# A transformer trunk layer on one core: projection weights split once and kept in DRAM, and the fillers' casts tied into order

## The chip, the cores and the metric

The kernel runs on one core of one Trainium2 chip. A core has five engines that work side by side, each on its own list of instructions, in the order of that list: PE (TensorE, matmuls), DVE (VectorE), ACT (ScalarE), POOL (GpSimd) and SP (SyncE), which here issues all DMAs. An engine that reaches an instruction whose inputs are not there, or whose output place is not free, waits, and what stands behind it on that engine waits too. The metric is the device time of one execution in microseconds (us); the median of several runs is compared.

## What is computed

One layer of an encoder over 1024 positions of width 1024 in float32. A combined projection gives queries, keys and values for two branches of eight heads (64 wide) and two gates. Branch a is softmax attention over a band with a learned bias, branch b is stick-breaking attention. Each branch is projected from 512 to 1024, gated by a sigmoid, the two are added and go through an output projection. Then come a residual with layer norm, a SwiGLU feed-forward part and a second layer norm.

```python
h = x @ w_in[l]
qa, ka, va, qb, kb, vb, ga, gb = jnp.split(h, split_pts, axis=-1)
y_a = chunk_band_attention(heads_a(qa), heads_a(ka), heads_a(va), rel_bias[l]) @ w_proj_a[l]
y_b = stick_breaking_attention(heads_b(qb), heads_b(kb), heads_b(vb)) @ w_proj_b[l]
gate_a = jax.nn.sigmoid(ga + b_gate[l, :D])
gate_b = jax.nn.sigmoid(gb + b_gate[l, D:])
mix = (gate_a * y_a + gate_b * y_b) @ w_out[l]
x = layer_norm(DEEPNORM_ALPHA * x + mix, ln1_g[l], ln1_b[l])
```

## The kernel before

**Precision.** Every float32 matmul is made of three faster ones. An operand is split into a high part (a cast, always on ACT) and a low part (source minus high part, on DVE or POOL); the products high x high, high x low and low x high are added in PSUM. So a weight costs a load, a cast on ACT and a subtraction before PE can use it. `begin_w` issues the load of a weight; the function that it returns, `end`, does the cast (L441, tiles wh_...) and the subtraction (L442, tiles wl_...).

**Stage one** (to about 345 us) makes the column blocks of the combined projection in pairs ("projects" p1 to p16), each with seven products in place of eight (Strassen's scheme). Queries, keys, values and five pairs of gates go to DRAM. ACT copies each product out of its PSUM bank and adds the gates' bias and sigmoid (L398), SP stores the result (L399). `run_pairs` runs the projects and loads the weights of the next ones ahead.

**The attention** (345 to about 663 us) goes over 16 heads, eight of branch a and then eight of branch b, of 12 steps each. For a head, PE makes scores (sc, L547 and L548), ACT, DVE and POOL make weights of them (branch a: exponentials L590, scale L595 on POOL; branch b: sigmoids L622 and L623, scans L625 and L628 on DVE, product L630 on POOL), PE transposes the weights (tp, L653), ACT and DVE split them (pt, L109 and L110), and PE multiplies them with the values (pv, L666 and L667). A group of four or eight steps shares one pv bank, of which there is one; when the group's last product is made, ACT copies the bank out (L685), and the next group may begin. `pend` holds products back by LAG = 2 steps.

Since a head's chain leaves PE with gaps, other matmuls, the **fillers**, are strewn between: `fill_all` is a generator that gives one matmul at a time, and the table FILL says how many of them each head's steps take. The fillers are the gates 10 to 15 (gps, L462), each with its own weight, and then the projection of branch a's heads (yAps, L738), whose inputs y0 to y3 are read back from DRAM and split (L774 on ACT, L775 on POOL) and whose weights (wr_y0_0 to wr_y0_3, raw) are loaded, cast and split in the midst of the heads. Gates that were not squashed in stage one are squashed (sigmoid, L782) when their tile comes up.

**The merge** (to about 708 us) multiplies branch b's heads with their projection weights (yBps, L116 to L119, two banks), multiplies by the gate (L880), adds branch a's part (L881) and splits the sum (mh, ml). Then comes the output projection (ops), whose first four weights o0_0 to o0_3 are loaded, cast and split beforehand; and then the feed-forward part, which the change doesn't touch.

**Order.** The program is written in one order, and a scheduler of the tile framework makes each engine's list of it; casts of weights drift ahead of their place in the program as early as it sees fit. An instruction given to `tc.keep_in_program_order` isn't moved. Tiles lie in numbered slots by tag (`op` has 8, `gt` 3, `kp` 4, `xt` 16); a tile that takes a slot waits until the last user of the slot before is done.

## Time and profile before

| What | Value |
|---|---|
| Median of 3 runs | 1456.3 us (1455.09 to 1456.57) |
| Profiled execution | 1452.42 us, of which the span in the profile is 1450.6 us |
| PE busy | 1429.1 us (99%), 6748 matmuls |
| DVE, ACT, POOL busy | 1024.0 us (71%), 678.7 us (47%), 279.2 us (19%) |
| DMA | 246.15 MB, mean 170 GB/s |

The profile is that of one execution. Matmuls overlap one another, so PE counts as busy also where it goes at less than its pace; a 128x512 matmul shows 389 ns, but one starts every 0.23 us where PE isn't held up. Rows of the timeline give start and duration in us, engine, line, tiles, and in brackets the idle time of the engine before the row with what ended it. Line numbers are those of the kernel before; the changed kernel has the same statements some lines further down.

### The profile page before, as it was taken

Reading aid. Unit: us, or ns where it says so; the run is one execution under the profiler, and the core shown is the slowest. Engines: PE = TensorE matmul, PEld = TensorE weight load, DVE = VectorE, ACT = ScalarE, POOL = GpSimd, SP = SyncE. Lnnn points to the kernel's source line nnn. Section 1 sums busy time; section 2 is a strip of 40 time slices with the busy share of each in tenths; the row PEclk is TensorE's granted clock in tenths of the full one; section 3 lists DMA queues with packets and bytes.
Section 4 is the critical chain, followed back from the end, with each engine's and each line's share of the span. In section 5 each row is a group of like instructions: output and inputs, shape, how many; then the busy total and the mean of one; then the engine's idle time right before and its main releaser. Section 6 shows DMA issues by size and latency. Waiting matters only on the chain.

```text
span 1450.6 us, 19152 instructions
## 1 busy us (share of the span) xinstructions
PE 1429.1 (99%) x6748; PEld 1182.6 (82%) x6748; DVE 1024.0 (71%) x1645; ACT 678.7 (47%) x1186; POOL 279.2 (19%) x326
## 2 busy tenths in 40 slices
PE   9999999999999998999999999999999999999997
PEld 7888888888888887887788888888888888888886
DVE  8875565434777776977848966766777765988767
ACT  6444444446887786774313633444444433221201
POOL 0000000003555888760005000000000000100016
PEclk9999999999999999999999999999999999999999
DMA  7555545338676566746502133444444457787602
GB/s 247 154 181 175 174 146 184 110 104 257 179 220 194 173 193 196 219 160 249 194 29 82 51 114 110 154 160 160 153 152 148 151 204 252 290 307 242 205 15 102
DMA packets 83167, 246.15 MB, mean 170 GB/s; under 512 B 10480, under 2 KB 10480, under 8 KB 83072
## 3 DMA queue, kind: packets, MB, share of 16 engines
q1 hardware_dynamic: 83072, 244.94, 50.8%
q8 instruction: 53, 0.87, 0.2%
q14 instruction: 42, 0.34, 0.1%
HBM read 161.51 MB, written 79.72 MB: 166 GB/s over the span
## 4 chain that ended last, share of the span: by engine, by line
PE 90%; DVE 4%; ACT 2%; DMA 2%; issue 1%; POOL 0%; SPq 0%; POOLq 0%; DVEq 0%; ACTq 0%
PE sxf L179 16%; PE sxp L179 12%; PE szf L179 8%; PE dx L1187 6%; PE szp L179 6%; PE syf L179 4%; PE gps L462 4%; PE dz L1187 3%; PE syp L179 3%; PE yAps L738 2%; PE tp_b L653 2%; PE ops L117 2%; PE ops L119 2%; PE ops L116 2%; PE tp_a L653 2%; PE fpswh_h L117 2%
## 5 line engine op out<-in xcount | busy, mean ns | idle before, releaser
L1143 POOL TENSOR_TENSOR wdyt<-wdyt 128x512 f32<-128x512 f32 x8 | 11.2, 1396 | 512.2 <-ACT h L1016 422.5
L630 POOL TENSOR_TENSOR w_b<-w_b,kp_b 128x511 f32<-128x511 f32 (+3 forms) x96 | 97.1, 1023 | 32.5 <-DVE kp_b L625 18.3
L625 DVE TENSOR_TENSOR_SCAN kp_b<-kp_b,ident_ps 128x512 f32<-128x512 f32 (+2 forms) x64 | 56.4, 883 | 31.8 <-ACT kp_b L622 31.5
L896 POOL TENSOR_TENSOR mv<-mv,neghalf 128x1 f32<-128x1 f32 x16 | 23.9, 1495 | 210.1 <-DVE mv L895 210.1
L565 POOL MEMSET bias<- 64x64 f32 x8 | 1.2, 145 | 328.0 <-ACT bias L564 328.0
L622 ACT ACTIVATE kp_b<-sc_b 128x512 f32<-128x512 f32 (+3 forms) x96 | 48.0, 500 | 27.9 <-PE sc_b L548 25.5
L194 DVE TENSOR_TENSOR c<-sxp,c 128x512 f32<-128x512 f32 x16 | 11.1, 691 | 69.8 <-issue 40.2
L110 DVE TENSOR_TENSOR pt_b<-tp_b,pt_b 128x512 fp32r<-128x512 f32 (+1 forms) x96 | 50.1, 543 | 8.7 <-ACT pt_b L109 8.0
L179 PE MATMUL szf<-x1S63h,wcf 128*128 128x512 f32 x168 | 55.1, 389 | 0.0
L1118 DVE TENSOR_TENSOR x<-dx,x 128x512 f32<-128x512 f32 x64 | 43.4, 686 | 14.9 <-PE dx L1187 14.9
L110 DVE TENSOR_TENSOR sl<-h,sl 128x512 fp32r<-128x512 f32 x56 | 38.4, 685 | 18.8 <-ACT sl L109 18.8
L110 DVE TENSOR_TENSOR pt_a<-tp_a,pt_a 128x512 fp32r<-128x512 f32 (+1 forms) x96 | 45.3, 486 | 8.8 <-ACT pt_a L109 7.7
L595 POOL TENSOR_SCALAR w_a<-w_a,st_a 128x640 f32<-128x640 f32 (+2 forms) x64 | 42.6, 671 | 41.3 <-DVE st_a L594 24.0
L109 ACT CAST sl<-h 128x512 fp32r<-128x512 f32 x56 | 34.7, 620 | 33.5 <-PE syf L179 17.1
L117 PE MATMUL ops<-wl_o,mh 128*128 128x512 f32 x128 | 50.1, 391 | 0.0
L116 PE MATMUL ops<-wh_o,mh 128*128 128x512 f32 x128 | 49.9, 390 | 0.0
L119 PE MATMUL ops<-wh_o,ml 128*128 128x512 f32 x128 | 49.9, 390 | 0.0
L653 PE MATMUL tp_b<-ident,w_b 128*128 128x128 f32 x288 | 47.9, 275 | 1.8 <-DVE pt_b L110 1.8
L590 ACT ACTIVATE w_a<-w_a,st_a 128x640 f32<-128x640 f32 (+2 forms) x64 | 44.5, 696 | 10.6 <-DVE st_a L584 8.8
L109 ACT CAST pt_b<-tp_b 128x512 fp32r<-128x512 f32 (+1 forms) x96 | 46.6, 497 | 5.7 <-PE tp_b L653 5.5
L1016 ACT ACTIVATE h<-sxf 128x512 f32<-128x512 f32 x21 | 12.6, 598 | 76.7 <-PE sxf L179 76.7
L623 ACT ACTIVATE w_b<-sc_b 128x511 f32<-128x511 f32 (+3 forms) x96 | 48.1, 501 | 0.0
(1889 smaller groups left out, 4833.9 us busy)
## 6 DMA issues: line engine op xcount, KB each, us to landing
s_dr<-sl SPq DMA_DIRECT2D x112, 256.0 KB, 2.3
sd<-s_dr SPq DMA_DIRECT2D x56, 512.0 KB, 4.7
wLf<-in_w_ffn_in_dram SPq DMA_DIRECT2D x22, 512.0 KB, 4.2
wRf<-in_w_ffn_in_dram SPq DMA_DIRECT2D x22, 512.0 KB, 3.5
wRp<-in_w_in_dram SPq DMA_DIRECT2D x17, 512.0 KB, 5.0
wLp<-in_w_in_dram SPq DMA_DIRECT2D x17, 512.0 KB, 5.6
v_dr<-v SPq DMA_DIRECT2D x16, 512.0 KB, 4.4
kl<-k_dr SPq DMA_DIRECT2D x32, 256.0 KB, 5.2
```

The source lines that it names most:

```text
L109: nc.scalar.copy(dst_h, src)
L110: nc.vector.tensor_tensor(dst_l, src, dst_h.bitcast(F32), ALU.subtract)
L116: mm(acc, lh, rh, start=(i == 0), stop=False)
L117: mm(acc, lh, rl, start=False, stop=False)
L119: mm(acc, ll, rh, start=False, stop=(i == n))
L179: mm(acc, lw[:, ks], rx, start=(first and kt == i == 0), stop=(kt == 3 and i == 2), skip_group_check=not first)
L462: mm(acc[hf], lw[:, ks], rx[k][:, (LO, HI)[hf]], start=(k == j == 0), stop=(k == KT - 1 and j == 2))
L623: nc.scalar.activation(be[:, m0:e], sc[:, m0 - c0:n], AF.Sigmoid)
L625: nc.vector.tensor_tensor_scan(kp[:, 0:e], kp[:, 0:e], ident_ps()[:, 0:e], 0.0, ALU.mult, ALU.add)
L630: nc.gpsimd.tensor_tensor(be[:, m0:e], be[:, m0:e], kp[:, m0 - 1:e - 1], ALU.mult)
L653: tr(tp[:, (qb - lo_q) * P:(qb - lo_q + 1) * P], wt[qb - q0][:, (kb - qb) * P:(kb - qb + 1) * P], ident)
L1187: mm(acc, a, b, start=(first and i == n == 0), stop=(i == n - 1 == 1), skip_group_check=not first)
```

## The change

- **Weights.** In stage one, after each of the last eight projects, `store_proj` loads one of the eight projection weights (two DMAs of 256 KB), casts it on ACT, subtracts on DVE and stores both halves in DRAM (two DMAs of 512 KB). It takes its tiles from the slots of queries, keys and values. Later `begin_proj` loads the two halves as they are (wyh..., wyl...), with no cast and no subtraction. This holds for the fillers' four weights (whose subtraction was POOL's) and the merge's four (DVE's); the merge's are loaded one step ahead, in `next_w`.
- **Ties.** The casts and subtractions of the gate weights, of y, and the late sigmoids are kept in program order.
- **y by halves.** `split_y` takes half a tile; the second halves are done later, at the gate's last steps and in the first filler of the projection.
- **FILL.** Five cells change; the sum stays 480.
- **pend.** In branch a the last product of a group is now made at the start of the second step of the next group; before, the products were held back one step longer at the third.
- **Output weights.** o0_0 to o0_3 are begun with the merge tiles n = 3 to 6 and split with n = 4 to 7, one each.

Three places in the engines' lists. First ACT in the fourth head of branch b (b3), where gate 15 ends and the projection fillers begin; kp_b and w_b are the sigmoids that empty a score bank. Before:

```order
L623 ACTIVATE w_b3_1_1_5601<-sc_b3_6_0_5646 128x255
L109 CAST pt_b3_0_4_5659<-tp_b3_0_4_5654 128x512
L441 CAST wh_y0_2_6218<-wr_y0_2_6041 128x1024
L622 ACTIVATE kp_b3_7_5667<-sc_b3_7_0_5669 128x128
L623 ACTIVATE w_b3_1_1_5601<-sc_b3_7_0_5669 128x127
L109 CAST pt_b3_0_5_5681<-tp_b3_0_5_5676 128x512
```

The same place now:

```order
L109 CAST pt_b3_0_4_5747<-tp_b3_0_4_5742 128x512
L485 COPY gate15_5402<-gps15_1_5404 128x512
L803 CAST yh1_5579<-yraw1_5479 128x512
L641 ACTIVATE kp_b3_7_5769<-sc_b3_7_0_5771 128x128
L642 ACTIVATE w_b3_1_1_5688<-sc_b3_7_0_5771 128x127
L109 CAST pt_b3_0_5_5783<-tp_b3_0_5_5778 128x512
```

The cast of the third projection weight, two tiles ahead of its use, is gone, and a half-wide cast of y1, whose first half was cast before, stands there.

Second DVE in the sixth and seventh heads of branch b (b5 and b6), around the product of a gate with yAps3. Before:

```order
L110 TENSOR_TENSOR pt_b5_0_3_6364<-tp_b5_0_3_6359,pt_b5_0_3_6364 128x512
L442 TENSOR_TENSOR wl_y1_3_7029<-wr_y1_3_7025,wh_y1_3_7028 128x1024
L110 TENSOR_TENSOR pt_b5_0_2_6376<-tp_b5_0_2_6372,pt_b5_0_2_6376 128x384
L625 SCALAR_TENSOR_TENSOR kp_b6_2_6384<-kp_b6_2_6384,ident_ps_4551 128x320
L741 TENSOR_TENSOR gA3_6044<-yAps3_1_6320,gA3_6044 128x512
```

Now:

```order
L110 TENSOR_TENSOR pt_b5_0_3_6456<-tp_b5_0_3_6451,pt_b5_0_3_6456 128x512
L110 TENSOR_TENSOR pt_b5_0_2_6468<-tp_b5_0_2_6464,pt_b5_0_2_6468 128x384
L766 TENSOR_TENSOR gA3_6133<-yAps3_1_6383,gA3_6133 128x512
L644 SCALAR_TENSOR_TENSOR kp_b6_2_6485<-kp_b6_2_6485,ident_ps_4636 128x320
L647 SCALAR_TENSOR_TENSOR kp_b6_2_6485<-kp_b6_2_6485,ident_ps_4636 128x448
```

The subtraction for the merge's first weight stood between two splits that PE waits for, and is gone.

Third ACT in the sixth head of branch a (a5), where its first group ends. Before:

```order
L109 CAST pt_a5_1_7_4205<-tp_a5_1_7_4200 128x512
L590 ACTIVATE w_a6_0_3_4075,st_a6_3_4188<-w_a6_0_3_4075,st_a6_3_4188 128x640
L109 CAST pt_a5_1_6_4216<-tp_a5_1_6_4212 128x384
L685 COPY yv_a5_0_4222<-pv_a5_0_4102 128x512
L109 CAST pt_a5_1_5_4238<-tp_a5_1_5_4235 128x256
```

Now:

```order
L109 CAST pt_a5_1_7_4289<-tp_a5_1_7_4284 128x512
L609 ACTIVATE w_a6_0_3_4153,st_a6_3_4272<-w_a6_0_3_4153,st_a6_3_4272 128x640
L704 COPY yv_a5_0_4298<-pv_a5_0_4173 128x512
L109 CAST pt_a5_1_6_4305<-tp_a5_1_6_4301 128x384
L109 CAST pt_a5_1_5_4322<-tp_a5_1_5_4319 128x256
```

The copy of the pv bank stands one cast earlier.

The diff, cut to its core:

```diff
...
 LAG = 2
 LEAD = ((6, 8, 9, 9, 10, 10, 11, 11, 12, 12, 13, 13), (7, 8, 9, 9, 10, 10, 11, 11, 12, 12, 13, 14))
-FILL = (22, 18, 18, 18, 18, 18, 18, 28, 42, 42, 42, 40, 40, 40, 38, 38)
+FILL = (18, 18, 18, 18, 18, 18, 18, 36, 42, 42, 40, 40, 40, 38, 38, 38)
...
         return pair_steps(f"p{i}", Wa[i], ops_x, c, done, "pv" if i == 3 else "mm")
+    def aside_work(i):
+        if i == 2:
+            small_inputs()
+        if i >= len(work) - 9:
+            store_proj(i - len(work) + 9)
+
     def run_pairs(steps, left, right, also=lambda i: None, first=2, aside=lambda i: None,
                   then=lambda: None):
...
         for cs, src in srcs:
             dma(r[:, cs], src)
-        def end():
+        def end(tied=False):
             hi = hl(f"wh_{name}", F32R)
             lo = hl(f"wl_{name}", F32R)
-            nc.scalar.copy(hi, r)
-            lo_eng.tensor_tensor(lo, r, hi.bitcast(F32), ALU.subtract)
+            for ins in (nc.scalar.copy(hi, r),
+                        lo_eng.tensor_tensor(lo, r, hi.bitcast(F32), ALU.subtract)):
+                if tied:
+                    tc.keep_in_program_order(ins)
             return hi, lo
         return end
     def load_w(*args):
         return begin_w(*args)()
+
+    wp_dr = [dram(f"wp_dr{i}_", 2) for i in range(8)]
+
+    def store_proj(i):
+        br, cc = divmod(i, 4)
+        take = lambda name, dtype=F32: cycle(QKV, name, dtype)
+        srcs = [(cs, w_proj[2 * cc + j][:, br * HW:(br + 1) * HW])
+                for j, cs in enumerate((LO, HI))]
+        for d, t in zip(wp_dr[i], load_w(srcs, f"proj{i}", take, take, nc.vector)):
+            dma(d, t.bitcast(F32))
     def of(tag):
         return lambda name, dtype=F32: slot(tag, name, dtype)
...
                 for k in (6, 7):
                     yield from part(hf, k)
                 take(hf)
+                freed(6 + hf)
         dma(g_dr[i], gt)
     def left_again(i):
...
     run_pairs([project(i) for i in range(1, len(work))],
               lambda i: left(i + 1) if i > 2 else left_again(3) if i == 2 else None,
-              lambda i: right(i + 1), first=3, then=rest_of_start, also=lambda i: small_inputs() if i == 2 else None)
+              lambda i: right(i + 1), first=3, then=rest_of_start, also=aside_work)
     first_gate = 2 * N_GATE
     first_w = begin_gate(first_gate, nc.vector)()
...
                             nc.gpsimd.tensor_tensor(yt[r, gs], yt[r, gs], yv[r, gs], ALU.add)
                             if h == 1 and g == 1:
                                 if hd["i"] > 4:
-                                    later.append([6, lambda: split_y(hd["i"], yt, nc.gpsimd, True)])
+                                    for n, cs in ((6, LO), (8, HI)):
+                                        later.append([n, lambda cs=cs: split_y(hd["i"], yt, cs)])
                                 else:
                                     dma(y_dr[hd["i"]], yt)
                         later.append([3, add])
...
         got = []
         for i in range(first_gate, 15):
             end = begin_gate(i + 1, nc.gpsimd)
-            yield from gate(i, w, lambda: got.append(end()))
+            yield from gate(i, w, lambda: got.append(end(True)))
             w = got.pop()
-        end = begin_proj(0, 0, "op", nc.gpsimd)
+        end = begin_proj(0, 0)
         ends = {}
+        pieces = []
+
         def freed(k):
-            if k == 0:
-                got.append(end())
             if k < 4:
-                ends[k] = begin_y(k, nc.gpsimd)
-            if k > 1:
-                ends.pop(k - 2)()
+                ends[k] = begin_y(k)
+            if 1 < k < 6:
+                ends[k - 2](LO)
+                pieces.append(lambda: ends[k - 2](HI))
+            elif k > 5:
+                pieces.pop(0)()
         yield from gate(15, w, lambda: None, freed)
-        w = got.pop()
+        w = end()
         gates = {0: begin_gA(0)}
         for cc in range(4):
             if cc < 3:
-                end = begin_proj(0, cc + 1, "op", nc.gpsimd)
+                end = begin_proj(0, cc + 1)
             for j in range(2):
                 c = 2 * cc + j
                 t = gates.pop(c)
...
                             mm(acc, lw[:, ks], rx[k][:, cs], start=(k == n == 0),
                                stop=(k == 3 and n == 2))
                             yield 1.0
+                        if k % 2 and pieces:
+                            pieces.pop(0)()
                     nc.vector.tensor_tensor(t[:, cs], acc, t[:, cs], ALU.mult)
                 if c < KEEP:
                     dma(m_dr[c], t)
                 else:
                     kept[c] = t
                 if c == 0:
-                    end_y = begin_y(4, nc.gpsimd)
-                elif c == 1:
-                    end_y()
+                    end_y = begin_y(4)
+                elif c < 3:
+                    end_y((LO, HI)[c - 1])
             if cc < 3:
                 w = got.pop()
-    def begin_proj(br, cc, raw, eng):
-
-        return begin_w([(cs, w_proj[2 * cc + j][:, br * HW:(br + 1) * HW])
-                        for j, cs in enumerate((LO, HI))], f"y{br}_{cc}", of(raw), of("op"), eng)
+    def begin_proj(br, cc):
+
+        hl = [slot("op", f"wy{p}{br}_{cc}", F32R) for p in "hl"]
+        for d, t in zip(wp_dr[4 * br + cc], hl):
+            dma(t.bitcast(F32), d)
+        return lambda: hl
     def begin_gA(c):
         t = slot("gt", f"gA{c}")
...
     KEEP, kept = 5, {}
     yh, yl = [None] * 8, [None] * 8
-    def begin_y(i, eng):
+    def begin_y(i):
         raw = slot("op", f"yraw{i}")
         dma(raw, y_dr[i])
-        return lambda: split_y(i, raw, eng)
-
-    def split_y(i, raw, eng, in_order=False):
-        yh[i] = slot("xt", f"yh{i}", F32R)
-        yl[i] = slot("xt", f"yl{i}", F32R)
-        for ins in (nc.scalar.copy(yh[i], raw),
-                    eng.tensor_tensor(yl[i], raw, yh[i].bitcast(F32), ALU.subtract)):
-            if in_order:
-                tc.keep_in_program_order(ins)
+        return lambda cs: split_y(i, raw, cs)
+
+    def split_y(i, raw, cs):
+        if yh[i] is None:
+            yh[i] = slot("xt", f"yh{i}", F32R)
+            yl[i] = slot("xt", f"yl{i}", F32R)
+        hi, lo = yh[i][:, cs], yl[i][:, cs]
+        tc.keep_in_program_order(nc.scalar.copy(hi, raw[:, cs]))
+        tc.keep_in_program_order(
+            nc.gpsimd.tensor_tensor(lo, raw[:, cs], hi.bitcast(F32), ALU.subtract))
     def squash(t, c, br):
         col = br * 8 + c
         if c >= N_GATE:
-            nc.scalar.activation(t, t, AF.Sigmoid, bias=bg[:, col:col + 1])
+            tc.keep_in_program_order(
+                nc.scalar.activation(t, t, AF.Sigmoid, bias=bg[:, col:col + 1]))
     fill = fill_all()
     state = dict(t=0.0, done=False)
...
         hidx, pos = si // nhead, si % nhead
         if hidx < 14 and pos == 8:
             load_qk(heads[hidx + 2])
-        if hidx < 15 and pos == 4:
-            load_v(heads[hidx + 1])
+        if pos == 4:
+            if hidx < 15:
+                load_v(heads[hidx + 1])
+            else:
+                next_w = begin_proj(1, 3)()
+        if hd["br"] == 0 and st == LAG - 1 and len(pend) == LAG:
+            pend.pop(0)()
         while wi < min(hidx * 8 + LEAD[hd["br"]][pos], len(wunits)):
             wunits[wi]()
             wi += 1
...
         goal += FILL[hidx] / nhead
         fill_until(0.5 * (last + goal))
         pend.append(mult)
-        wait = hd["br"] == 0 and st == LAG
-        while len(pend) > LAG + wait:
+        if len(pend) > LAG:
             pend.pop(0)()
         fill_until(goal)
     for m_ in pend:
...
         mh.append(m_slot(f"mh{c}", F32R))
         ml.append(m_slot(f"ml{c}", F32R))
     acc_t = [slot(tag, f"acc{tt}") for tt, tag in enumerate(["pt"] * 4 + ["yt"] * 3 + ["bw"])]
+    wo_ends, wo = [], []
     for n, c in enumerate((6, 7, 5, 4, 0, 1, 2, 3)):
         if n % 2 == 0:
-            w = begin_proj(1, c // 2, "op", nc.vector)()
+            w = next_w
+            if n < 6:
+                next_w = begin_proj(1, (2, 0, 1)[n // 2])()
         gB = slot("kp", f"gB{c}")
         dma(gB, g_dr[2 * c + 1])
         squash(gB, c, 1)
...
             nc.vector.tensor_tensor(gB[:, cs], acc, gB[:, cs], ALU.mult)
             nc.vector.tensor_tensor(mA[:, cs], gB[:, cs], mA[:, cs], ALU.add)
             split(mh[c][:, cs], ml[c][:, cs], mA[:, cs])
+        if wo_ends:
+            wo.append(wo_ends.pop()(True))
+        if 2 < n < 7:
+            wo_ends.append(begin_w(w_out[(n - 3) * P:(n - 2) * P, :], f"o0_{n - 3}", of("gt"),
+                                   of("xt"), nc.vector))
     def bcast(src, t):
...
             pieces.pop(0)()
     for half_k in range(2):
-        wo = [load_w(w_out[(4 * half_k + j) * P:(4 * half_k + j + 1) * P, :], f"o{half_k}_{j}",
-                     of("gt"), of("xt"), nc.vector) for j in range(4)]
         if half_k == 1:
+            wo = [load_w(w_out[(4 + j) * P:(5 + j) * P, :], f"o1_{j}", of("gt"), of("xt"),
+                         nc.vector) for j in range(4)]
             left_f(0)
             R0 = slot("gt", "wRf0")
             dma(R0, w_ffn_in[NF])
```

## Prediction

> **What bounds the kernel now.** I read the page first, for PE's share of the span and the chain that ended last.
>
> ```profile
> span 1450.6 us, 19152 instructions
> PE 1429.1 (99%) x6748; PEld 1182.6 (82%) x6748; DVE 1024.0 (71%) x1645; ACT 678.7 (47%) x1186; POOL 279.2 (19%) x326
> PE 90%; DVE 4%; ACT 2%; DMA 2%; issue 1%; POOL 0%; SPq 0%; POOLq 0%; DVEq 0%; ACTq 0%
> ```
>
> TensorE (PE) is the bound, and the change touches no matmul: their number and shapes stay. So the time can only move by what PE stands still, and by its clock. Next come the windows, to see where PE has holes.
>
> ```profile
> 200.00:250.00 50.00, 50.00 (x230) 41.26 (x229) 29.87 (x39) 22.39 (x32) 0.00 (x0) 1.00 0.50 146
> 300.00:350.00 50.00, 49.99 (x226) 40.88 (x225) 18.43 (x37) 25.36 (x33) 6.57 (x10) 1.00 0.64 197
> 345.00:360.00 15.00, 14.70 (x83) 11.53 (x82) 10.95 (x46) 13.98 (x32) 8.19 (x12) 1.00 0.96 282
> 360.00:375.00 15.00, 14.26 (x92) 12.36 (x91) 12.56 (x51) 12.01 (x33) 9.44 (x14) 1.00 0.54 152
> 500.00:550.00 50.00, 50.00 (x285) 42.84 (x284) 38.23 (x54) 40.70 (x93) 42.29 (x50) 1.00 0.62 184
> 550.00:600.00 50.00, 45.51 (x247) 38.05 (x246) 37.72 (x55) 36.26 (x84) 39.81 (x52) 0.97 0.73 221
> ```
>
> The columns are stretch and length, then busy time of PE, PE's weight loads, DVE, ACT and POOL, then clock, DMA share and GB/s. In stage one (the first two rows) PE has no hole. The attention, from 345 on, has small ones, and 550 to 600 has one of 4.5 us with a lower granted clock. The waits of PE give names to the holes, and of ACT and SyncE's queue (SPq) the slack of stage one (192 to 345).
>
> ```profile
> PE sc_b L547 <- ACT w_b L623: 4.9, 2, 4.5
> PE tp_a L653 <- DVE pt_a L110: 1.1, 3, 0.5
> SPq L399 <- ACT c L398: 58.9, 8, 15.6
> ACT c L207 <- DMA wLp<-in_w_in_dram: 1.9, 1, 1.9
> ```
>
> Each row gives total, times, longest. A busy PE hides short waits, so the terms below are read from the timeline of each place.
>
> **Term 1, the cast of the projection weight in the fillers.** Of the timeline at 550:
>
> ```profile
> 550.16 0.80 SPq L436 DMA_DIRECT2D wr_y<-in_w_proj_dram  x2
> 553.73 1.04 ACT L441 CAST wh_y<-wr_y 128x1024 fp32r<-128x1024 f32 x1 [5.17 <-POOL w_b L630]
> 550.33 0.39 PE L548 MATMUL sc_b<-kl,qs 128*128 128x512 f32 x1
> 555.17 0.50 PE L547 MATMUL sc_b<-kh,qs 128*128 128x512 f32 x1 [4.46 <-ACT w_b L623]
> 559.15 0.60 PE L653 MATMUL tp_b<-ident,w_b 128*128 128x128 f32 x4
> 559.83 0.39 PE L666 MATMUL pv_b<-pt_b,v 128*128 128x512 f32 x1
> ```
>
> ACT works in order. It sat 5.17 us before this cast. POOL is named as releaser, but the load behind the cast was issued only at 550.16, and the cast began 3.57 us later: it waited for the landing. Behind it stood the sigmoids that empty the score bank, so PE stood 4.46 us. Afterwards its instructions last 0.60 instead of 0.39 until 559.83: 4.66 us x (1 - 0.39/0.60) = 1.6 us more, less the small part that is ordinary there. In the changed order a half-wide cast of y1 stands here, whose source was loaded a gate earlier; the weight's halves come ready from DRAM, and only PE waits for them, four products later. I take -6.0 (ends: -6.1, and 0 if another waits at the same place).
>
> **Term 2, the splits of the second branch's weights and the gate sigmoids.**
>
> ```profile
> 608.95 2.14 DVE L442 TENSOR_TENSOR wl_y<-wr_y,wh_y 128x1024 fp32r<-128x1024 f32 x1
> 611.70 0.30 PE L653 MATMUL tp_b<-ident,w_b 128*128 128x128 f32 x1 [0.35 <-DVE pt_b L110]
> 614.38 0.63 PE L653 MATMUL tp_b<-ident,w_b 128*128 128x128 f32 x4 [0.74 <-DVE pt_b L110]
> 637.46 1.20 DVE L442 TENSOR_TENSOR wl_y<-wr_y,wh_y 128x1024 fp32r<-128x1024 f32 x1
> 640.18 0.41 PE L653 MATMUL tp_b<-ident,w_b 128*128 128x128 f32 x2 [0.67 <-DVE pt_b L110]
> 651.33 1.15 ACT L782 ACTIVATE gB<-gB,bg 128x1024 f32<-128x1024 f32 x1 [3.62 <-DMA gB<-g_dr]
> 653.01 0.50 PE L666 MATMUL pv_b<-pt_b,v 128*128 128x512 f32 x1 [0.54 <-ACT pt_b L109]
> ```
>
> Twice a DVE subtraction stands ahead of the split that PE waits for, and the third time ACT waits 3.62 us for a gate to land and squashes it ahead of a cast. The subtractions go; the three gate sigmoids go behind the attention, into the merge, each tied ahead of its own tile. PE's idle time in these rows is 0.35 + 0.74 + 0.67 + 0.54 = 2.3 us. I take all of it: -2.3 (ends: -2.3 and 0).
>
> **Term 3, the merge.**
>
> ```profile
> 689.14 1.22 DVE L442 TENSOR_TENSOR wl_y<-wr_y,wh_y 128x1024 fp32r<-128x1024 f32 x1
> 691.61 0.50 PE L116 MATMUL yBps<-yh,wh_y 128*128 128x512 f32 x1 [0.98 <-DVE gB L880]
> ```
>
> DVE is behind because the last projection split and the output splits fall in a bunch. With the first gone and one output split per merge tile it keeps pace: -1.0. What is late next is the last output weight, whose load now waits for the first one's split and whose cast stands behind the last merge tile. A merge tile's chain (multiply, add, cast, cast of 1.05, subtraction of 1.2) ends about when PE has spent the 24 matmuls of 0.23 us that it can do first. I price that at +0.5 (0 to +1). The loads of the merge tiles' other halves move later in SyncE's queue, behind the end of the fillers; they are used from six products on (6 x 12 x 0.23 = 16.6 us), which hides a landing like the 3.6 us of term 1.
>
> **Term 4, the copy of pv.** In branch a the pv bank is one; each group's first product waits for ACT's copy of the group before.
>
> ```profile
> 363.06 0.47 PE L462 MATMUL gps<-xh,wh_g 128*128 128x512 f32 x1
> 363.74 0.50 PE L666 MATMUL pv_a<-pt_a,v 128*128 128x512 f32 x1 [0.20 <-ACT yt L685]
> 440.99 0.46 ACT L109 CAST pt_a<-tp_a 128x384 fp32r<-128x384 f32 x1
> 441.35 0.59 ACT L685 COPY yv_a<-pv_a 128x512 f32<-128x512 f32 x1
> 441.37 0.48 PE L462 MATMUL gps<-xh,wh_g 128*128 128x512 f32 x1
> 441.99 0.50 PE L666 MATMUL pv_a<-pt_a,v 128*128 128x512 f32 x1
> 457.06 0.48 PE L462 MATMUL gps<-xh,wh_g 128*128 128x512 f32 x1
> 457.63 0.50 PE L666 MATMUL pv_a<-pt_a,v 128*128 128x512 f32 x1
> ```
>
> The product starts 0.68, 0.62 and 0.57 us after the matmul before it, where 0.23 is the pace of such a matmul: 0.45, 0.39 and 0.34 lost. Seven such places lie between 363 and 458, the first and last shown. The new rule puts the copy ahead of the cast that it stands behind here, so 0.36 us earlier (441.35 - 440.99), and the last product of a group half a step earlier. That covers the wait: 7 x 0.33 = -2.3 (ends: -2.7 and 0).
>
> **Term 5, fillers.** At the start of the attention PE idles 0.30 + 0.74 us (345 to 375) with ACT at 13.98 of 15; two casts of 1.05 us leave this stretch. I take -0.5 (0 to -1.0). At the passage from branch a to b, eight more filler matmuls stand in the last head of a (36 for 28, 1.8 us of cover) against the 1.1 us for which tp_a waits: -0.5 (0 to -1.1). The other cells move two or four matmuls a head (0.5 to 0.9 us that PE does in any case), which I price at nothing.
>
> **Term 6, stage one.**
>
> ```profile
> L436 SPq DMA_DIRECT2D wr_y<-in_w_proj_dram x16: 327/424/781, 470.7 to 677.2; - x16
> L441 ACT CAST wh_y<-wr_y x8: 1045/1052/1082, 478.4 to 687.8; 128x1024 fp32r<-128x1024 f32 x8
> ```
>
> Durations in ns: least, median, most. Eight weights are now cast (8 x 1.05 = 8.4 us of ACT) and subtracted (8 x 1.20 = 9.6 us of DVE) over some 150 us, in which ACT is busy 22 to 25 of 50 and DVE 18 to 30. SyncE issues 32 DMAs more (16 raw loads, 16 stores, 32 x 0.42 = 13.6 us), and waits 58.9 us there for one line alone. Moved are 4 MB in and 8 MB out; later 8 MB are read where 4 MB were, so about 261 MB instead of 245. At 146 and 197 GB/s, 12 MB over 150 us add 80 GB/s, which stays below the 282 of the row at 345. Behind each new cast on ACT stands the copy that frees a PE bank. ACT's wait of 1.9 us for wLp shows that a late landing there left PE whole. So +0.3; the cover is the half-idle ACT, and if it fails a wait is priced like term 1.
>
> **Term 7, y in halves, and ties.**
>
> ```profile
> L109 ACT CAST yh<-yt 128x512 fp32r<-128x512 f32 x2 | 1.2, 622 | 1.5 <-DVE yt L674 1.5
> L442 POOL TENSOR_TENSOR wl_y<-wr_y,wh_y x4: 2367/2400/2415, 498.7 to 584.0; 128x1024 fp32r<-128x1024 f32 x4
> ```
>
> Two casts of 0.62 us for one of 1.05 cost ACT 0.19 us more, for seven tiles 1.3 us, beside other work (ACT's 40.7 of 50 from 500 to 550 covers it; uncovered it is 1.3 us). POOL loses four subtractions of 2.4 us. The ties keep a cast from drifting ahead, and a tied cast that is late holds up all behind it: +0.5 (0 to +2).
>
> **Sum.** -6.0 - 2.3 - 1.0 - 2.3 - 0.5 - 0.5 = -12.6; + 0.5 + 0.3 + 0.5 = +1.3; together -11.3 us. The profiled execution took 1452.4 us (span 1450.6), so it would take 1441.1. The median of the runs is 1456.3, 3.9 above it; I carry that distance over: 1445.0.
>
> **Rivals.**
> *The next wait takes over* (half the gain). In 550 to 600 POOL is busy 39.8 of 50 and DVE 37.7, so when ACT no longer waits, PE may wait for POOL's product or DVE's scan. For: the small holes have different releasers. Against: from 500 to 550 both were busier (42.3 and 38.2) and PE had no hole. Terms 2, 4 and 5 then give nothing: -6.0 - 1.0 + 1.3 = -5.7, 1450.6.
> *Stage one breaks* (slower). The raw load of a projection weight waits in SyncE's queue for a store or a slot, the new cast on ACT waits for it as in the row at 553.73, and the bank copies behind it stop PE. Each full one costs 6.1 us. It decides from two on (-11.3 + 12.2); at three, +18.3 - 11.3 = 7.0, 1463.3. For: a cast in order and a load issued just before it is exactly term 1's case, eight times. Against: SyncE's and ACT's slack above.
> *Nothing comes of it.* Tied casts in the heads wait instead of the removed ones (terms 1, 2 and 5 at 0, term 7 at its worst): -1.0 - 2.3 + 0.8 + 2.0 = -0.5, 1455.8.
> *More than forecast.* The same subtraction took 2.14 us at 608.95 and 1.20 at 637.46, so something held it for 0.94 us. If it was POOL, the four POOL subtractions that go free DVE as often: -3.8 more, 1441.2. The Trainium skill's page "SBUF — State Buffer", section "SBUF: two separate sides", says that DVE with two inputs in SBUF and GpSimd take a shared port pair as an exclusive lock, and the one that comes second stands for the other's whole instruction. By that rule these 0.94 us are POOL's, and the sum would be -15.1 rather than -11.3; but it also speaks against the change, since the halves of y stay on POOL and now fall among the busiest heads. The trace shows both lengths, not the lock, so I leave the sum as it is.
>
> **How the numbers follow.** Forecast 0.54 (its own range 1441 to 1449: the small terms at half or at their ends), more 0.08, half the gain 0.17, nothing 0.06, stage one breaks 0.15. About 0.2% (2.9 us) is what a measurement here can tell from no change. Faster: 0.54 + 0.08 + 0.14 of the 0.17 = 0.76. Same: the 0.03 left and half of 0.06 = 0.06. Slower: 0.15 + 0.03 = 0.18. The range 1437 to 1455 leaves out the slower case and the tails.
>
> **What would show it.** Right: no PE idle over 1 us from 345 to 700; ACT's longest wait for wh or yh under 1 us; 50.0 of 50 on PE from 200 to 350; clock 1.00 in 550 to 600. Wrong: ACT waiting for a wr_proj landing with PE holes in stage one; tp_b or sc_b waiting for POOL or DVE as long as before; a wait of ops for the last output weight above 1 us.

## The result, and the profile after

The changed kernel takes 1449.1 us (median of 5 runs, 1447.1 to 1449.6) against 1456.3 us of the kernel before, measured beside it: a ratio of 0.9951, with a 95% interval of 0.9936 to 0.9965. It is faster by 0.5%, 7.2 us. The profiled execution took 1448.6 us, 3.8 us less than the 1452.4 of the kernel before.

The page of the changed kernel, as far as it answers to the lines shown of the kernel before:

```profile
span 1446.8 us, 19239 instructions
PE 1428.1 (99%) x6748; PEld 1182.8 (82%) x6748; DVE 1029.5 (71%) x1649; ACT 679.5 (47%) x1193; POOL 269.2 (19%) x329
PE 93%; DVE 3%; ACT 1%; issue 1%; DMA 1%; POOL 0%; SPq 0%; POOLq 0%; DVEq 0%; ACTq 0%
```

PE's share of the chain of work that ended last rose from 90% to 93%; POOL has 10.0 us less to do, near the 9.6 us of the four subtractions taken from it. The windows of the same stretches (columns as before: stretch and length, busy time of PE, PE's weight loads, DVE, ACT, POOL, clock, DMA share, GB/s):

```profile
200.00:250.00 50.00, 50.00 (x230) 41.23 (x229) 30.34 (x39) 22.89 (x32) 0.00 (x0) 1.00 0.64 200
300.00:350.00 50.00, 49.88 (x225) 40.77 (x224) 20.85 (x40) 24.76 (x34) 2.40 (x7) 1.00 0.68 219
345.00:360.00 15.00, 14.43 (x88) 11.89 (x86) 11.29 (x47) 11.98 (x30) 5.93 (x11) 1.00 0.89 229
360.00:375.00 15.00, 14.33 (x91) 12.11 (x90) 12.32 (x48) 14.03 (x37) 11.41 (x14) 1.00 0.65 187
500.00:550.00 50.00, 50.00 (x283) 42.80 (x283) 38.47 (x55) 40.86 (x97) 39.50 (x54) 1.00 0.66 208
550.00:600.00 50.00, 46.58 (x255) 39.64 (x254) 38.28 (x55) 35.80 (x85) 36.74 (x51) 0.97 0.82 257
```

Stage one carries its new load (DMA share 0.64 where it was 0.50) without a hole on PE; the 0.12 us missing from 300 to 350 lie behind 345, where the attention begins. But 550 to 600 still has a hole of 3.4 us and a clock of 0.97, where 4.5 us and 0.97 stood before. The waits of PE from 340 on, and below them one of ACT and one of SyncE's queue in stage one:

```profile
PE yAps L761 <- POOL yl L805: 3.4, 1, 3.4
PE pv_a L685 <- ACT yt L704: 1.6, 4, 0.8
PE tp_b L672 <- DVE pt_b L110: 0.6, 2, 0.3
...
ACT wh_proj L447 <- DMA wr_proj<-in_w_proj_dram: 5.2, 5, 2.0
SPq L399 <- ACT c L398: 29.9, 9, 7.4
```

The wait of 4.9 us for the score bank is gone and tp_b waits 0.6 us, where its three places of term 2 had 1.8. Two waits are new or longer: a projection filler waits 3.4 us, once, for POOL's low half of y, and pv_a waits 1.6 us in four times for the copy of its bank, where the kernel before had 0.2 in one (term 4 meant to remove this wait). The timeline shows where the first comes from:

```profile
562.58 0.27 PE L672 MATMUL tp_b<-ident,w_b 128*128 128x128 f32 x1
566.27 0.65 PE L761 MATMUL yAps<-yl,wyh 128*128 128x512 f32 x1 [3.42 <-POOL yl L805]
567.78 0.63 PE L761 MATMUL yAps<-yh,wyh 128*128 128x512 f32 x1
...
557.87 1.30 POOL L805 TENSOR_TENSOR yl<-yraw,yh 128x512 fp32r<-128x512 f32 x1
561.43 1.29 POOL L708 TENSOR_TENSOR yt<-yt,yv_b 64x512 f32<-64x512 f32 x1 [2.26 <-DMA yv_b<-yt]
562.72 2.21 POOL L649 TENSOR_TENSOR w_b<-w_b,kp_b 128x383 f32<-128x383 f32 x2
564.96 1.25 POOL L805 TENSOR_TENSOR yl<-yraw,yh 128x512 fp32r<-128x512 f32 x1
```

POOL did the second half of y2 at 557.87. Next in its list stands the sum of yt5, which waits 2.26 us for a DMA, then two of branch b's products (w_b), and only then the second half of y3 (564.96 to 566.21), whose matmul PE had reached at about 562.8. While POOL sat idle for the DMA, the work that PE would need was behind it.

To put numbers on the small waits, which a busy PE hides, I add up the **lost pace**: for each matmul the time from its start to the next one's, less the usual time for that pair of shapes (the fastest quarter's). Another way to take the usual time for the same pairs shifts a sum by about 1 us, much alike in all kernels, so the differences between kernels are what counts. The table has the sums by stretches of the span, in us:

| Kernel | 325-375 | 375-475 | 475-550 | 550-600 | 600-675 | 675-750 | whole span |
|---|---|---|---|---|---|---|---|
| Before | 6.1 | 14.7 | 5.3 | 9.6 | 8.8 | 1.5 | 59.7 |
| Changed | 6.3 | 15.9 | 5.7 | 8.4 | 5.8 | 0.6 | 56.1 |

The 3.6 us that the sums differ by are the two spans' difference (3.8) within 0.2. Most of the gain of the profiled execution is in 600 to 675 (3.0); 550 to 600 gave 1.2 us where 6 were expected, and 375 to 475 lost 1.2.

The profile thus tells of 3.8 us, the medians of 7.2. The kernel before varies more from run to run (1451.5 to 1458.3 over the jobs below, without one run in a slow state that took 2032.6) than the changed one, and its profiled execution lies low in that spread. What makes its runs differ wasn't shown.

### The profile page after: what moved, and what is told of

It is laid out like the page before. It is cut to its first block, busy times and chain, and to the rows that moved or that the text cites. A ratio compares the mean times of both kernels' runs of the same rounds, so it can differ in the third digit from the quotient of the medians.

```text
span 1446.8 us, 19239 instructions
## 1 busy us (share of the span) xinstructions
PE 1428.1 (99%) x6748; PEld 1182.8 (82%) x6748; DVE 1029.5 (71%) x1649; ACT 679.5 (47%) x1193; POOL 269.2 (19%) x329
## 2 busy tenths in 40 slices
DMA packets 87777, 262.95 MB, mean 182 GB/s; under 512 B 10992, under 2 KB 10992, under 8 KB 87680
## 4 chain that ended last, share of the span: by engine, by line
PE 93%; DVE 3%; ACT 1%; issue 1%; DMA 1%; POOL 0%; SPq 0%; POOLq 0%; DVEq 0%; ACTq 0%
PE sxf L179 16%; PE sxp L179 11%; PE szf L179 8%; PE dx L1228 6%; PE szp L179 5%; PE syf L179 4%; PE gps L480 4%; PE syp L179 3%; PE dz L1228 3%; PE yAps L761 3%; PE tp_b L672 2%; PE ops L116 2%; PE ops L119 2%; PE ops L117 2%; PE tp_a L672 2%; PE fpswh_h L119 2%
## 5 line engine op out<-in xcount | busy, mean ns | idle before, releaser
L1057 ACT ACTIVATE h<-sxf 128x512 f32<-128x512 f32 x21 | 12.5, 597 | 77.1 <-PE sxf L179 77.1
```

## The experiments

Times are compared with the kernel before, run on the same chip in the same job; its median was 1453.9 to 1455.8 us there. Ratios stand with their 95% intervals. A ratio is not that of the two medians, so it and the difference of the medians can disagree by up to 0.8 us.

**The second halves earlier.** The changed kernel with one line edited:

```diff
-                        if k % 2 and pieces:
+                        if pieces:
                             pieces.pop(0)()
```

> The changed kernel with the second halves of y taken at every step of the first yAps product, not at every other one; so POOL's subtraction of y3's second half stands ahead of the sum of yt5 (which waits for a DMA) and of two products w_b. Theory: the 3.42 us for which PE waits in the changed kernel at 566 us comes from that place in POOL's list alone. Then PE's wait and the slower clock behind it go: 3.4 + about 1.1 = 4.5 us less than the changed kernel, about 1444.6. Rival: POOL is the bound there, whatever the order; the products w_b come later by the 1.25 us of the subtraction and PE waits for tp_b in its place: 1448 to 1450.

Measured: 1442.9 us, ratio 0.9929 (0.9917 to 0.9942), 11.0 below the kernel before. Two rows of POOL and the window of that stretch:

```profile
558.69 1.29 POOL L805 TENSOR_TENSOR yl<-yraw,yh 128x512 fp32r<-128x512 f32 x1
560.66 1.30 POOL L708 TENSOR_TENSOR yt<-yt,yv_b 64x512 f32<-64x512 f32 x1 [0.69 <-DMA yv_b<-yt]
...
550.00:600.00 50.00, 50.00 (x284) 42.66 (x283) 42.84 (x62) 39.96 (x94) 42.03 (x57) 1.00 0.90 277
```

The last half is done at 559.98, ahead of the sum, and PE has no hole: 284 matmuls' records in the 50 us where the changed kernel has 255, clock 1.00. Lost pace in 550 to 600 falls from 8.4 to 3.4 us, the span from 1446.8 to 1441.1. The theory held and the rival fell, though POOL is busy for 42.0 of 50. The place in POOL's list was the cause.

**Is it the tie or the place?** The changed kernel with POOL's subtraction untied:

```diff
-        tc.keep_in_program_order(
-            nc.gpsimd.tensor_tensor(lo, raw[:, cs], hi.bitcast(F32), ALU.subtract))
+        nc.gpsimd.tensor_tensor(lo, raw[:, cs], hi.bitcast(F32), ALU.subtract)
```

> The changed kernel with POOL's subtractions of y not tied (ACT's casts stay tied). In POOL's list y3's second half then still stands behind the sum of yt5, but ahead of the two products that it stands behind in the changed kernel. Theory: the place in the program, where the second half is asked for only at the fourth step, makes the wait, and the tie adds the part of those two products (2.2 us): PE waits about 1 us instead of 3.4, with less of a slow clock behind, 1445 to 1446 (9 to 10 below the kernel before). Rival: the tie is all of it, and the wait goes (11 below). Second rival: nothing changes (7 below).

Measured: 1447.6 us, ratio 0.9951 (0.9938 to 0.9965), 7.4 below. The second rival. PE waits as before:

```profile
PE yAps L761 <- POOL yl L804: 3.2, 1, 3.2
```

The expectation had the list wrong: in this kernel too y3's second half stands behind the sum and both products. So the tie isn't what put it there; the program asks for that half only at the fourth step of the first yAps product, and the scheduler left it where it was asked for.

**Stage one's part alone.** The kernel before with `store_proj` after each of the last eight projects and nothing else:

```diff
...
+        if i >= len(work) - 9:
+            store_proj(i - len(work) + 9)
...
-              lambda i: right(i + 1), first=3, then=rest_of_start, also=lambda i: small_inputs() if i == 2 else None)
+              lambda i: right(i + 1), first=3, then=rest_of_start, also=aside_work)
```

> The kernel before with the eight projection weights loaded, cast, subtracted and stored in DRAM in stage one, and the stored halves then never read: the price of stage one's part by itself (16 raw loads, 8 casts, 8 subtractions, 16 stores more). Theory: it costs nothing, PE stays whole from 200 to 350: 1456.3 within 1.5. Rival: casts on ACT wait for landings and PE stands: 1458 or more, with PE holes in stage one.

Measured: 1454.3 us, ratio 1.0005 (0.9996 to 1.0015). Its busiest window in stage one, and the old wait of PE, still there:

```profile
250.00:300.00 50.00, 50.00 (x222) 41.43 (x221) 27.75 (x36) 26.05 (x35) 0.00 (x0) 1.00 0.73 263
...
PE sc_b L563 <- ACT w_b L639: 5.0, 2, 4.5
```

Sixteen loads, sixteen stores, eight casts and eight subtractions cost nothing there that can be told from the noise (0.15% at most), with the DMA share at 0.73. The rival with late landings fell: ACT does wait for them (2.5 us in three times here, 5.2 in five in the changed kernel), and PE is whole, 45.00 of 45 us from 300 to 345 as well.

**The weights from DRAM alone.** That kernel with `begin_proj` reading the stored halves:

```diff
...
-        return begin_w([(cs, w_proj[2 * cc + j][:, br * HW:(br + 1) * HW])
-                        for j, cs in enumerate((LO, HI))], f"y{br}_{cc}", of(raw), of("op"), eng)
+        hl = [slot("op", f"wy{p}{br}_{cc}", F32R) for p in "hl"]
+        for d, t in zip(wp_dr[4 * br + cc], hl):
+            dma(t.bitcast(F32), d)
+        return lambda: hl
```

> The kernel before with the projection weights made in stage one and read from DRAM as halves, and nothing else of the change: y whole, no ties, old table, old merge but for its weights. Theory: this part carries the gain; the wait at 550 and the DVE subtractions at 609, 637 and 689 go, 6 + 2 + 0.5 us: 1447 to 1449. Rival: the wait is only handed on, and the ties, halves or the merge's order make the gain: 1452 to 1456.

Measured: 1443.3 us, ratio 0.9932 (0.9917 to 0.9947), 10.7 below the kernel before. More than the whole change gains. The window, and PE's largest waits from 340 on:

```profile
550.00:600.00 50.00, 49.94 (x281) 42.40 (x280) 43.13 (x62) 37.69 (x89) 38.63 (x52) 1.00 0.81 259
...
PE tp_a L669 <- DVE pt_a L110: 1.1, 3, 0.5
PE tp_b L669 <- DVE pt_b L110: 0.7, 2, 0.4
PE sc_b L563 <- ACT w_b L639: 0.7, 2, 0.5
```

No single wait of PE over 0.5 us is left from 340 to 715. Here y is split whole, during the gate, as before, and is ready in time: the last of POOL's five subtractions for tiles read back from DRAM begins at 549.27 and takes 2.40 us.

**All but the weights from DRAM.** The changed kernel with the weights loaded raw, cast and split at their place, and no `store_proj`:

```diff
...
-        hl = [slot("op", f"wy{p}{br}_{cc}", F32R) for p in "hl"]
-        for d, t in zip(wp_dr[4 * br + cc], hl):
-            dma(t.bitcast(F32), d)
-        return lambda: hl
+        return begin_w([(cs, w_proj[2 * cc + j][:, br * HW:(br + 1) * HW])
+                        for j, cs in enumerate((LO, HI))], f"y{br}_{cc}", of("op"), of("op"),
+                       (nc.gpsimd, nc.vector)[br])
```

> The changed kernel without the weights from DRAM: loaded raw, cast and subtracted at their place as before, all else of the change kept. Theory: the weights carry the gain, and the rest costs: slower than the kernel before, by 0 to 6 us, with ACT or PE waiting for raw weights and for yl at 550 to 570. Rival: the ties, halves and the new orders gain by themselves, 3 to 7 us below the kernel before.

Measured: 1453.4 us, ratio 0.9986 (0.9977 to 0.9996), 2.3 below. Neither the theory (slower) nor the rival's 3 to 7: the rest of the change is worth a little by itself, 0.14%. PE's largest waits:

```profile
PE yAps L759 <- POOL wl_y L446: 3.1, 1, 3.1
PE pv_b L683 <- ACT yt L702: 2.3, 1, 2.3
PE yAps L759 <- POOL yl L802: 1.7, 1, 1.7
```

The wait for the score bank has turned into one for the weight's low half, and the wait for yl is there as well. The parts don't add: the weights alone give 0.68%, the rest alone 0.14%, both together 0.49%.

**The late sigmoids.** The run with the weights from DRAM, with only the tie of the sigmoids added, which puts the three gate sigmoids into the merge:

```diff
-            nc.scalar.activation(t, t, AF.Sigmoid, bias=bg[:, col:col + 1])
+            tc.keep_in_program_order(
+                nc.scalar.activation(t, t, AF.Sigmoid, bias=bg[:, col:col + 1]))
```

> The kernel before with the projection weights from DRAM and the late sigmoids tied into the program's order, and nothing else. In the run with the weights from DRAM alone, PE still waits 0.3 + 0.2 us at 644 for pt_b, whose cast stands behind gate sigmoids on ACT. Theory: with them in the merge this goes, 1 us less than with the weights alone, 11.5 below the kernel before. Rival: nothing more than the weights alone (10.7 below), since the next wait takes over.

Measured: 1442.6 us, ratio 0.9908 (0.9891 to 0.9924), 13.2 below. Lost pace in 600 to 675 falls from 6.2 to 5.4 us, as expected, while the profiled spans are equal (1441.3 and 1441.1), since 375 to 475 was worse by 1.5 us in this execution. The interval overlaps that of the weights alone, so this shows the loss of pace there smaller and no more.

**The rule for a group's last product.** Four kernels. First the changed kernel with the old rule:

```diff
-        if hd["br"] == 0 and st == LAG - 1 and len(pend) == LAG:
-            pend.pop(0)()
...
-        if len(pend) > LAG:
+        wait = hd["br"] == 0 and st == LAG
+        while len(pend) > LAG + wait:
             pend.pop(0)()
```

> The changed kernel with the old rule for the last product of a group (held back one step longer). Theory: the new rule gains nothing, since the copy of the pv bank still stands behind an exponential and the next group's first product comes earlier too; 1449 within 1.5. The prediction's term 4 says 2.3 us slower, 1451.4. A rival, that the new rule harms (windows from 375 to 475 lost 1.2 us more than before), says about 1448.

Measured: 1445.5 us, ratio 0.9948 (0.9936 to 0.9961), 8.4 below the kernel before; the changed kernel was 7.2 below. The prediction's 2.3 us aren't there. PE's wait for yl is 2.4 us in this kernel and 3.4 in the changed one, so the 1.2 us are not the rule's alone. The waits of pv_a for the copy yt (1.6 us) are gone with the old rule, and waits of tp_a (1.0 us in place of 0.4) and sc_a (0.5) stand in their place.

Then the same edit on top of the earlier halves:

> The changed kernel with y's second halves at every step (as in the run of the pieces) and the old rule for a group's last product. Theory: the new rule costs about 1 us (stretches 375 to 475: 15.1 us of lost pace with it, 14.3 without), so this is 1 us below the run of the pieces alone: 12 us below the kernel before. Rivals: the rule does nothing (11 below), or it gains the 2.3 us of term 4, and this is 9 below.

Measured: 1442.4 us, ratio 0.9909 (0.9894 to 0.9923), 13.4 below. With the new rule the same kernel had 0.9929 (0.9917 to 0.9942); the intervals overlap a little, the two ran on different chips, and the profiled spans are 1440.8 and 1441.1. That the new rule costs is likely and not shown; that it gains 2.3 us is refuted.

Third, the new rule on the kernel with weights from DRAM and tied sigmoids:

> The kernel before with the weights from DRAM, the late sigmoids tied, and the change's rule for products. Theory: it gains nothing or costs up to 1 us: 10 to 11.5 below the kernel before, with pv_a waiting for the copy in the waits as in the changed kernel. The prediction's term 4 says 2.3 us gained.

Measured: 1443.1 us, ratio 0.9924 (0.9911 to 0.9937), 11.7 below. Nothing gained, again. And fourth, to see why, the early last product together with the old holding back of the first:

```diff
+        if hd["br"] == 0 and st == LAG - 1 and len(pend) == LAG:
+            pend.pop(0)()
         while wi < min(hidx * 8 + LEAD[hd["br"]][pos], len(wunits)):
```

> The kernel before with the weights from DRAM, the late sigmoids tied, and of the rule for products both halves: the last product of a group early (as in the change) and the first of the next group held back (as before), so 2.5 steps between them in place of 2 (before) and 1.5 (changed). Theory: the pv wait is set by that distance, and the change failed to shorten it because it brings the first product forward as well; here the seven or so waits of pv_a for ACT's copy go, 2 us less than the same kernel without it (about 13 below the kernel before). Rival: PE then stands for another member of branch a's chain (tp_a, sc_a), nothing gained: 11 below.

Measured: 1442.3 us, ratio 0.9913 (0.9900 to 0.9927), 12.5 below. The place at 441 of the prediction's term 4, in this kernel:

```profile
441.96 0.48 PE L478 MATMUL gps<-xh,wh_g 128*128 128x512 f32 x1
442.27 0.40 PE L682 MATMUL pv_a<-pt_a,v 128*128 128x512 f32 x1
...
PE tp_a L669 <- DVE pt_a L110: 1.1, 3, 0.5
PE tp_b L669 <- DVE pt_b L110: 0.7, 2, 0.4
```

The first product of the group starts 0.31 us after the matmul ahead of it, where it was 0.62 in the kernel before and in the run with the tied sigmoids, on which this one builds. The waits for ACT's copy are gone, and with them 1.4 us of lost pace on pv_a from 375 to 475 (7.6 to 6.2, against that run). But the scores, sc_a, lose 1.7 us more (2.9 to 4.6), and the time is the same. Half the theory held: the distance sets the wait. The rival held on the time: what pv_a no longer loses in branch a, PE loses at the scores.

**The table of fillers.** The run with early halves and the old rule, with the old FILL as well:

> The same with the old table of fillers as well, so that only the weights from DRAM, the ties, the halves and the merge's order are left of the change. Term 5 says that the new table gains 1 us: then this is 1 us slower than the run before it. Theory: the table does nothing (0 within 0.7).

Measured: 1442.3 us, ratio 0.9909 (0.9894 to 0.9924), the same as without. And the new table on the kernel with weights from DRAM and tied sigmoids:

> The kernel before with the weights from DRAM, the late sigmoids tied, and the change's table of fillers. Theory: the table does nothing within 0.7 us: 11 below the kernel before. The prediction's term 5 says 1 us gained, half of it at the passage from branch a to b, where tp_a's waits for DVE would fall from 1.1 us.

Measured: 1443.2 us, ratio 0.9918 (0.9904 to 0.9931), 11.6 below. Its waits show the trade:

```profile
PE pv_a L682 <- ACT yv_a L701: 1.1, 2, 0.6
PE tp_b L669 <- POOL w_b L631: 1.0, 1, 1.0
...
PE tp_a L669 <- DVE pt_a L110: 0.4, 1, 0.4
```

tp_a's waits for DVE fall from 1.1 to 0.4 us, as term 5 said, and waits of pv_a and tp_b come in their place: lost pace falls by 1.9 us in 375 to 475 (15.8 to 13.9) and rises by 2.2 in 475 to 550 (5.5 to 7.7).

The best kernels of this study take the weights from DRAM and either split y whole as before with the sigmoids tied (0.9908), or do y's halves early with the old rule (0.9909). Both beat the changed kernel by about 6 us. Since the first has whole y, no other ties, the old table, the old rule and the old order of the output weights, none of these parts of the change adds a gain that could be seen beside the weights from DRAM (the intervals are 4 to 5 us wide).

## Why the prediction was right, and where it was wrong

The prediction said 1445.0 us, 1437 to 1455, and faster with a chance of 0.76; measured were 1449.1 and faster. The direction and the range held. The forecast's own range, 1441 to 1449, just missed, and the case that came true is nearest to the rival *the next wait takes over* (1450.6): it named POOL as the next to be waited for, though for its score product and not for y's low half. Two of the prediction's own signs of being right failed: PE has an idle stretch of 3.42 us between 345 and 700, where it allowed 1, and the clock in 550 to 600 is 0.97 and not 1.00. The other two held: PE is whole from 200 to the end of stage one (of the last 50 us, which reach into the attention, 49.88), and ACT's longest wait for a wh or yh from 345 on is 0.8 us. By its steps:

- **What bounds the kernel.** Right. PE's matmuls are the same 6748, and the time moved by what PE lost in pace.
- **Term 1 (-6.0).** The price was right, the change didn't collect it. With the weights from DRAM alone, lost pace in 550 to 600 falls from 9.6 to 3.6 us, 6.0 to the tenth. In the changed kernel it falls to 8.4 only: -1.2. The row of 0.60 us at 559.15 with which the prediction shows the slow clock is four transposes together, which take 0.62 us at 548.73 too, ahead of the hole; the matmuls of 128x512 between 557.0 and 558.7 bear the reading out, with 0.60 to 0.63 in place of 0.39.
- **Term 7 (+0.5, at worst +2) is the step that failed.** It looked at y's halves as ACT time and at ties as casts that come late on ACT. What counted was when POOL does the last half. It cost 8.4 - 3.4 = 5.0 us of lost pace, the 3.42 us of waiting and the slow clock behind it (matmuls of 0.63 us until about 569.3). The prediction priced POOL's work and not its place in the list.
- **Term 2 (-2.3).** Right: 600 to 675 lost 8.8 us before and 5.8 in the changed kernel, -3.0; 2.6 of it come with the weights alone, 0.8 with the sigmoids.
- **Term 3 (-1.0, and +0.5).** Right: 675 to 750 went from 1.5 to 0.6. The wait for the last output weight did not show. The weights alone bring this stretch to 0.3, so the output weights' new order wasn't needed for it.
- **Term 4 (-2.3).** Wrong, +1.2 in the changed kernel (375 to 475). The copy moved ahead of one cast, but it still stands behind an exponential that waits for DVE, and the new rule brings the next group's first product forward too:

```profile
440.61 0.83 ACT L609 ACTIVATE w_a<-w_a,st_a 128x640 f32<-128x640 f32 x1 [0.53 <-DVE st_a L603]
441.43 0.56 ACT L704 COPY yv_a<-pv_a 128x512 f32<-128x512 f32 x1
441.41 0.48 PE L480 MATMUL gps<-xh,wh_g 128*128 128x512 f32 x1
442.05 0.50 PE L685 MATMUL pv_a<-pt_a,v 128*128 128x512 f32 x1 [0.16 <-ACT yv_a L704]
```

  0.64 us between the last two, where 0.62 stood before. The prediction took 0.23 us for the pace of a product that isn't held up; the run with both halves of the rule shows 0.31 at these places. Over the twelve changes of group from 375 to 465, the interval ahead of the first product adds up to 5.5 us before and 5.8 in the changed kernel: it is shorter at six of them (0.47 to 0.31 at 447), about the same at two and longer at four (0.31 to 0.64 at 426, 0.57 to 1.17 at 458). And the waits don't add up to time: with all of them gone, nothing is gained.
- **Term 5 (-1.0).** Wrong by its size: the windows at 345 and 360 idle 0.57 + 0.67 = 1.24 us where it was 1.04, and the table, tried by itself, only moves the loss.
- **Term 6 (+0.3).** Right; by itself stage one's part costs 0.05% (-0.04 to 0.15%). The DMAs of the changed kernel move 262.95 MB where 246.15 were; the prediction's 261 and 245 are 1 to 2 MB low. The rival *stage one breaks* is refuted.
- ***More than forecast.*** The lock between DVE and POOL, of which the Trainium skill's page "SBUF — State Buffer" speaks in its section "SBUF: two separate sides", was to free 3.8 us more. The eight subtractions in stage one, where POOL is idle, take 1.22 us each, in keeping with it. POOL's list in the kernel before agrees at both places that the prediction compares:

```profile
607.74 2.26 POOL L630 TENSOR_TENSOR w_b<-w_b,kp_b 128x383 f32<-128x383 f32 x2
634.58 0.88 POOL L630 TENSOR_TENSOR w_b<-w_b,kp_b 128x319 f32<-128x319 f32 x1 [1.08 <-DVE kp_b L625]
637.69 1.70 POOL L630 TENSOR_TENSOR w_b<-w_b,kp_b 128x319 f32<-128x319 f32 x1 [0.72 <-ACT w_b L623]
```

  DVE's subtraction of 608.95 began while POOL's product ran (until 610.00), and took 2.14 us. That of 637.46 was first and took 1.20; there POOL's product, begun at 637.69, took 1.70 where its like takes 0.88. But the rival's gain wasn't to be had: beside POOL's four subtractions (498.7 to 586.4 us) every DVE instruction took its usual time. And the weights from DRAM alone gain 10.7 us, which terms 1, 2 and 3 (9.3) nearly fill. No experiment tried the lock itself.
- **The step from the profile to the median.** The 3.9 us between the profiled execution and the median of before were carried over. They belong to the kernel before: for the changed kernel the distance is 0.5 us.

Terms 4, 5 and 7 were off by 3.5, 1.2 and 4.5 us against the change, and the carried distance by 3.4 us for it, so the forecast is nearer to the result than its terms deserve. For the profiled execution it said 1441.1 and 1448.6 came, 7.5 us off; that the median came within 4.1 us is in part luck.

## What to carry to other kernels

Where work is taken off one engine in order, read the lists of all the engines that feed the same consumer: the wait moves to whatever is late next, and on an in-order engine that is set by the place in the list, above all behind an instruction that waits for a DMA. Split a tile by halves only if the last half is asked for as early as the whole was. Small waits of one chain that are all paid by the same engine don't add up: take one away and see whether the time moves before counting all.

## What the runs showed of the hardware

After the hole of 3.42 us PE's 128x512 matmuls lasted 0.63 us in place of 0.39 and the granted clock of 550 to 600 was 0.97, as after the hole of 4.46 us before. The changed kernel with the old rule for products has the same after a hole of 2.40 us: matmuls of 0.63 us for 3.0 us, clock 0.97. After the many holes under 1 us, in kernels with a clock of 1.00 there, nothing of that kind was seen; one of 0.98 us, in the merge of the kernel before, is followed by matmuls of 0.39. The loss beside the hole was about the same for all three lengths: 1.6 us after 4.46 (the prediction's sum), 1.6 after 3.42 (5.0 of lost pace less 3.4), and about 1.6 after 2.40 (lost pace of 550 to 600 about 7.4, against 3.4 with the earlier halves, less the 2.4). And 263 GB/s with a DMA share of 0.73 beside a PE without a hole (250 to 300 in stage one) left nothing to see in the time of the added 12.6 MB (258.75 MB moved, 246.15 before).
